# SSD scan: the outputs of two stages issued together, halves first, then carried states

## The chip, the cores and the metric

The kernel runs on one core of one Trainium2 chip. The metric is the device time of one execution in microseconds (us), as the median of several runs. The profile is one execution, recorded by the hardware profiler. Engines are named as there: PE is TensorE's matmul, PEld its weight load, DVE is VectorE, ACT ScalarE, POOL GpSimd, SP SyncE, whose queue issues most transfers.

## What is computed

One inference step of a two-layer streaming encoder, in float32, for 1024 prompt frames and 64 sample frames. Layer 0 is a Mamba-2 SSD mixer with a SwiGLU FFN, layer 1 banded attention with a SwiGLU FFN. The change touches the scan in the mixer alone. Cut to the scan, the reference is:

```python
CB = jnp.einsum('bcqgn,bcsgn->bcgqs', Cc, Bc)
y_diag = jnp.einsum('bcgjqs,bcsgjp->bcqgjp', CB[:, :, :, None] * Lm, xd)
chunk_states = jnp.einsum('bcsgn,bcsgjp->cbgjpn', Bc, xd * decay_to_end[..., None])
# scan over chunks: h -> h * chunk_decay + chunk_state; h_prev is the state ahead of each chunk
y_off = jnp.einsum('bcqgn,cbgjpn->bcqgjp', Cc, h_prev) * jnp.moveaxis(jnp.exp(Acs), -1, 2)[..., None]
y = (y_diag + y_off).reshape(b, L, SSM_HEADS, P)
```

After that come the skip term D, the gate silu(z), a norm for each of four groups, and the output projection.

## The kernel before

Frames lie along the free dimension: 1088 frames are three slices of 384, 384 and 320, and a slice is three chunks of up to 128. The 2048 inner channels are 16 tiles j of 128, two heads of 64 in each. One stage of the scan is a tile and a slice, q = 3 j + s, 48 stages in all.

PE's order is the program's order. It is written by a planner, the class Stream: the main line emits units of the input projection (24 matmuls mm for one weight tile and one slice, in two parts), and after each part a pump lets the side tasks run that are due. The planner has its own clock st.t, to which every unit and every step of a side task adds an estimated cost; a step is due after a delay and when a condition holds. `st.wait_for` lets that clock run on, without matmuls, until a condition holds. The other engines and SP's queue are ordered by the framework's scheduler.

A stage is the side task ssd_task(j, s), begun when the unit x of its tile and slice is out. Its steps are:

- load: MT and ea come from the decay rows in memory (L814, L817); DVE and ACT turn them into decays (L823 to L825). It needs C >= q - 3.
- A: three transposes xtp (L835), xd on DVE (L845), xe on POOL (L846), and MT times CB (L847). It needs C >= q - 1 and a gap of SSD_GAP = 4.4 after the last A.
- B, 6.0 later: six matmuls sp (L854), six updates hn of the carried state on DVE (L864, L867).
- C, 3.5 later: the outputs. Products of halves yp (L884, 12 matmuls in the profile, each 64 columns of the array, the two heads in the two halves), the products with the carried states yo (L893, six matmuls of 128 columns, four in the first stage of a tile), then y on DVE (L895), ea on DVE (L897), their sum on POOL (L898).
- D: y times z (L905), the transfer to memory (L906), squares for the norm. It needs z of the stage, and D in order.

The counters so["A"] to so["D"] hold how many stages have passed each step. The main line waits on them as well: unit x of stage q for C > q - 5, unit z for D > q - 3, unit C of a group for C. table_task (L683 to L713) makes the decay rows once, ahead of the first stage. PSUM has eight banks: two for mm, two for the small products (ax), four in the pool pyy for yp and yo. Buffers rotate by tag: xd 2, ea 3, h 6, y 6, halo 6.

Of the kernel before, what the change touches and what calls it, by code (L numbers as in the profile page):

```python
# [8 lines left out]
F32 = mybir.dt.float32  # L9
# [3 lines left out]
ALU = mybir.AluOpType  # L13
# [3 lines left out]
P = 128  # L17
D = 1024
# [5 lines left out]
SL = [(0, 384), (384, 384), (768, 320)]  # L24
# [5 lines left out]
CHL = [128] * 8 + [64]  # L30
# [15 lines left out]
SSD_GAP, SSD_D = 4.4, 8.0  # L46
# [35 lines left out]
C_D = 208  # L82
# [292 lines left out]
def hybrid_kernel(  # L375
# [5 lines left out]
    V, A, G, PE = nc.vector, nc.scalar, nc.gpsimd, nc.tensor  # L381
    ctx.enter_context(tc.manual_schedule(engines={mybir.EngineType.PE}))
    st = Stream()
# [49 lines left out]
    def col(c):  # L433
        return pcs[:, c:c + 1]
# [203 lines left out]
    with ExitStack() as es:  # L638
        pyy = es.enter_context(tc.tile_pool(reuse_waits="tile", name="pyy", bufs=4, space=PSUM))
        sb1 = es.enter_context(tc.tile_pool(reuse_waits="tile", name="sb1", bufs=1))  # L640
        sb2 = es.enter_context(tc.tile_pool(reuse_waits="tile", name="sb2", bufs=2))
# [33 lines left out]
        def table_task():  # L675
            ps = ax("dtn")
            for c in range(NCH):
                PE.matmul(ps[:, c * 32:(c + 1) * 32], dtT[c // 3][:64, (c % 3) * P:(c % 3 + 1) * P], stk, start=True, stop=True)
            with tc.high_priority(HIP):
                tt_ = [sb2.tile([P, 3, P], F32, tag=tg, bufs=2, name="tt") for tg in ("xe", "xe")]  # L680
                t0, t1 = (fl(t_)[:, :HW].rearrange("p (a b) -> p a b", b=HEADS) for t_ in tt_)
                t3 = dec
                V.tensor_tensor(t0, ps[:, :HW].rearrange("p (a b) -> p a b", b=HEADS), hb(pbs[:, 0:32]), op=ALU.add)  # L683
                V.scalar_tensor_tensor(fl(t1), fl(t0), -1.0, fl(t0), op0=ALU.mult, op1=ALU.min)
                A.activation(fl(t1), fl(t1), AF.Exp)
                V.tensor_scalar(fl(t3), fl(t1), LP[-1], None, op0=ALU.mult)
                for c_ in LP[-2::-1]:
                    V.scalar_tensor_tensor(fl(t3), fl(t3), c_, fl(t1), op0=ALU.add, op1=ALU.mult)
                V.scalar_tensor_tensor(fl(dt), fl(t0), 0.0, fl(t3), op0=ALU.max, op1=ALU.add)
                V.memset(dt[64:128, 8, :], 0.0)  # L690
                V.tensor_tensor(t0, dt, hb(negA), op=ALU.mult)
            yield 1.0, TB_V
            pa = ax("acsp")
            PE.matmul(pa[:, :HW], U, fl(t0), start=True, stop=True)
            with tc.high_priority(HIP):
                V.tensor_copy(fl(nac), pa[:, :HW])
            yield 0.5, 1.0
            pl_ = ax("lastp")
            PE.matmul(pl_[:, :HW], ones, fl(t0), start=True, stop=True)

            with tc.high_priority(HIP):
                for s, (o, n) in enumerate(SL):
                    ps = pyy.tile([P, 512], F32, tag="yy", name="acT")
                    for i in range(3):
                        c = 3 * s + i
                        L = CHL[c]
                        PE.transpose(ps[:32, i * P:(i + 1) * P], nac[:, c, :], ident)
                    row = sb2.tile([P, 384], F32, tag="xd", name="row")
                    A.copy(row[:32, :], ps[:32, :384])
                    nc.sync.dma_start(ac_[:, o:o + 384], row[:32, :])  # L710
                V.tensor_tensor(fl(dec), fl(nac), pl_[:, :HW], op=ALU.subtract)
                A.activation(fl(cd), pl_[:, :HW], AF.Exp, scale=-1.0)
                A.activation(fl(dec), fl(dec), AF.Exp)  # L713
            yield 1.7, 2.5
            tabs.append(1)
# [15 lines left out]
        class Conv:  # L731
# [5 lines left out]
            def __call__(self, s, ps_):  # L737
                ct = self.ct
                dst = self.dst[s] = sb2.tile([P, 384], F32, tag=self.tag, bufs=self.bufs, name=self.tag)
                raw = sb2.tile([P, 390], F32, tag="craw", bufs=4, name="craw")  # L740
                if s == 0:
                    G.memset(raw[:, 0:3], 0.0)
                else:
                    G.tensor_copy(raw[:, 0:3], self.prev[:, 0:3])
                if s < 2:
                    w_ = 384
                    scaled(raw[:, 3:387], ps_, s, 0, 384)
                    self.prev = sb2.tile([P, 4], F32, tag="halo", bufs=6, name="halo")
                    G.tensor_copy(self.prev[:, 0:3], raw[:, 384:387])
                else:  # L750
                    w_ = 323
                    G.tensor_copy(raw[:, 259:262], scs[:, ct, :])
                    scaled(raw[:, 3:259], ps_, s, 0, 256)
                    scaled(raw[:, 262:326], ps_, s, 256, 64)
                    G.tensor_copy(cst[:, ct, 0:3], raw[:, 256:259])
                    G.tensor_copy(cst[:, ct, 3:6], raw[:, 323:326])

                cw = C_CW + ct * 4
                A.activation(dst[:, :w_], raw[:, 0:w_], AF.Identity, bias=col(C_CB + ct), scale=col(cw))
                for k in range(1, 4):  # L760
                    V.scalar_tensor_tensor(
                        dst[:, :w_], raw[:, k:k + w_], col(cw + k), dst[:, :w_], op0=ALU.mult, op1=ALU.add
                    )
                if s < 2:
                    A.activation(dst[:, :384], dst[:, :384], AF.Silu)
                else:
                    A.activation(dst[:, 0:256], dst[:, :256], AF.Silu)
                    A.activation(dst[:, 256:320], dst[:, 259:323], AF.Silu)  # L768
                    A.activation(dst[:, 320:384], ident[:, 0:64], AF.Copy, scale=0.0)
# [30 lines left out]
        cb_done = []  # L800
        hst = {}
        so = dict(A=0, B=0, C=0, D=0, tA=0, tC=0)
        ssgs = {}

        def ssd_task(j, s):
            g, jj = divmod(j, 4)
            xsT = pair_t[j].dst[s]
# [4 lines left out]
            MT = sb2.tile([P, 2, 384], F32, tag="bp", bufs=4, name="MT")  # L812
            row = ac_.offset + 2 * j * NCH * P + o
            nc.sync.dma_start(MT, bass.AP(ac_.tensor, row, [[0, P], [NCH * P, 2], [1, 384]]))  # L814
            ea = sb2.tile([P, 384], F32, tag="ea", bufs=3, name="ea")
            for e in range(2):
                nc.sync.dma_start(ea[64 * e:64 * e + 64, :n], bass.AP(ac_.tensor, row + e * NCH * P, [[0, 64], [1, n]]))  # L817
            m3 = MT[:, :, :n]
# [5 lines left out]
            A.activation(m3, m3, AF.Exp, scale=-1.0)  # L824
            x = A.activation(ea[:, :n], ea[:, :n], AF.Exp, scale=-1.0)  # L825
            tc.add_manual_dep(x.ins, last.ins.name, AT, reason="one table load")
            yield 0, SSD_D, lambda: (g, s) in cb_done and so["A"] == q and so["C"] >= q - 1 and st.t >= so["tA"]
            Bn, CB = bc_t[g, s]
            if s == 2:
                h0 = sb2.tile([P, P], F32, tag="h0", bufs=1, name="h0")  # L830
# [2 lines left out]
            pt = ax("xtp")  # L833
            for i in range(3):
                PE.transpose(pt[:, i * P:(i + 1) * P], xsT[:, i * P:(i + 1) * P], ident)  # L835
            xd = sb2.tile([P, 3, P], F32, tag="xd", name="xd")
            xe = sb2.tile([P, 3, P], F32, tag="xe", name="xe")

            def hd(ap):
# [16 lines left out]
            for i in range(3):  # L856
# [2 lines left out]
                    hst[j] = h0  # L859
                h = hst.get(j)  # L860
                hs.append(h)
                hn = sb2.tile([P, P], F32, tag="h", bufs=6, name="hn")
                if c == 0:
                    V.tensor_copy(hn, sp[:, :P])  # L864
                else:
# [9 lines left out]
                if c == 8:  # L875
                    nc.sync.dma_start(hs_o[:, j * P:(j + 1) * P], hn)
            so["B"] = q + 1
            yield 0.8, 3.5, lambda: so["C"] == q and so["D"] >= q - 5 and st.t >= so["tC"]

            yp = pyy.tile([P, 512], F32, tag="yy", name="yp")  # L880
            for i in range(3):
                L = CHL[3 * s + i]
                for e in range(2):
                    PE.matmul(  # L884
                        yp[64 * e:64 * e + 64, i * P:i * P + L], xd[:, i, 64 * e:64 * e + 64],
                        MT[:, e, i * P:i * P + L], start=True, stop=True,
                    )
            yo = pyy.tile([P, 512], F32, tag="yy", name="yo")
            for i in range(3):
                c = 3 * s + i  # L890
                L = CHL[c]
                if c > 0:
                    PE.matmul(yo[:, i * P:i * P + L], hs[i], CT[:, i * P:i * P + L], start=True, stop=True)  # L893
            y = sb2.tile([P, 384], F32, tag="y", bufs=6, name="y")
            V.scalar_tensor_tensor(y[:, :n], xsT[:, :n], col(C_D + j), yp[:, :n], op0=ALU.mult, op1=ALU.add)  # L895
            q0 = P if s == 0 else 0
            V.tensor_tensor(ea[:, q0:n], yo[:, q0:n], ea[:, q0:n], op=ALU.mult)  # L897
            G.tensor_tensor(y[:, q0:n], y[:, q0:n], ea[:, q0:n], op=ALU.add)  # L898
            so["C"] = q + 1
            so["tC"] = st.t + SSD_GAP  # L900
            yield 1.5, 0, lambda: (j, s) in zst and so["D"] == q
            so["D"] = q + 1

            end = V if j == XT - 1 else G
# [50 lines left out]

        xss, done = [], []
        ssg0 = sb2.tile([P, NCH * P], F32, tag="ssg", bufs=1, name="x0")
        tags = [[], [("bp", 4)] * 4 + [("y", 6)] * 3 + [("ea", 3)], [("ea", 3)] + [("CT", 5)] * 2 + [("xd", 2)] * 2]
        for s, (o, n) in enumerate(SL):
            xs = []  # L960
            if s == 0:
# [1023 lines left out]
```

## Time and profile before

| what | value |
|---|---|
| median of 3 runs | 2992.34 us (2991.45 to 2995.91) |
| profiled execution | 2995.14 us, span 2993.4 us |
| mean granted clock of PE | 0.993 |
| DVE, ACT, POOL busy over the span | 68%, 48%, 24% |
| stages of the scan on PE, first xtp to last yo | 97.25 to 671.84 us, 48 stages |
| matmuls yp, yo, sp, xtp | 576, 256, 288, 144 |

Instructions of one kind in a row are merged in the timeline into one line with a count (x12); the first number is the start, the second the time to the end of the last. Idle time stands in brackets with what ended it; "issue" is time in which the engine waited for nothing that the profile shows. The ends of matmuls are modelled, so distances are taken from start to start.

### The profile page before, as it was taken

The page shows a single profiled execution, that of the slowest core. Times are in us where ns is not written, and L with a number is a line of the kernel's source. Part 1 is how long each engine was busy: PE and PEld are TensorE (multiplying, and loading weights), DVE is VectorE, ACT ScalarE, POOL GpSimd, SP SyncE. Part 2 cuts the span into 40 slices and gives each one's busy share as a digit, 9 for nine tenths or more (in the row PEclk, how much of TensorE's full clock was granted, in tenths as well). Part 3 has the DMA queues.
Part 4 walks back from the last instruction along what each step waited for, and adds up shares of the span by engine and source line. Part 5 has one row for each costly group of instructions (what it writes and reads, how often), then busy time and mean ns, then how long its engine had stood idle before and what let it go on. Part 6 is the DMA issues. An engine that isn't in the chain of part 4 may idle for free.

```text
span 2993.4 us, 56388 instructions
## 1 busy us (share of the span) xinstructions
PE 2935.9 (98%) x21626; PEld 2878.7 (96%) x21626; DVE 2039.4 (68%) x4471; ACT 1450.9 (48%) x2574; POOL 709.0 (24%) x821
## 2 busy tenths in 40 slices
PE   8899999999999999999999999999999999999999
PEld 7899999999999999999999899999999999999999
DVE  7788887876768554574557777777778655475544
ACT  6675666654453232244445566555654322244443
POOL 1233333330121433351111000000131343452111
PEclk9999999999999999999999999999999999999999
DMA  3333333334654222255655322222356222245654
GB/s 122 99 108 95 103 98 105 95 102 150 187 147 144 84 73 80 76 161 173 203 177 168 88 83 73 69 65 85 123 166 187 80 75 77 80 149 174 214 180 136
DMA packets 201550, 363.36 MB, mean 121 GB/s; under 512 B 20544, under 2 KB 149280, under 8 KB 201280
## 3 DMA queue, kind: packets, MB, share of 16 engines
q1 hardware_dynamic: 199488, 353.39, 38.1%
q0 software_dynamic: 1792, 6.36, 1.1%
q8 instruction: 170, 2.79, 0.4%
q14 instruction: 100, 0.82, 0.1%
HBM read 292.47 MB, written 62.74 MB: 119 GB/s over the span
## 4 chain that ended last, share of the span: by engine, by line
PE 83%; DVE 9%; DMA 4%; ACT 2%; issue 2%; POOL 0%; SPq 0%; DVEq 0%; ACTq 0%; POOLq 0%
PE px L1263 9%; PE px L1265 9%; PE px L1264 9%; PE mm L454 7%; PE mm L456 7%; PE mm L455 7%; PE po L1463 6%; PE po L1464 6%; PE po L1462 6%; PE mmx L455 3%; PE mmx L454 3%; PE mmx L456 3%; PE po L1746 2%; PE ptp L1707 1%; PE yp L884 1%
## 5 line engine op out<-in xcount | busy, mean ns | idle before, releaser
L454 PE MATMUL mm<-r,hl 128*128 128x384 f32 (+2 forms) x1664 | 557.9, 335 | 5.5 <-ACT BT L768 3.0
L456 PE MATMUL mm<-r,hl 128*128 128x384 f32 (+2 forms) x1664 | 540.3, 325 | 3.6 <-DVE hl L353 2.8
L455 PE MATMUL mm<-r,hl 128*128 128x384 f32 (+2 forms) x1664 | 539.2, 324 | 0.0
L341 DVE TENSOR_TENSOR hl<-raw,hl 128x1024 fp32r<-128x1024 f32 (+1 forms) x219 | 260.9, 1192 | 222.6 <-ACT hl L340 218.6
L1264 PE MATMUL px<-r,hl 128*128 128x288 f32 (+1 forms) x1184 | 347.6, 294 | 0.0
L454 PEld LDWEIGHTS mm<-r,hl 128*128 128x128 f32 x1664 | 316.1, 190 | 7.5 <-ACT BT L768 3.2
L456 PEld LDWEIGHTS mm<-r,hl 128*128 128x128 f32 x1664 | 315.2, 189 | 5.0 <-DVE hl L353 3.9
L455 PEld LDWEIGHTS mm<-r,hl 128*128 128x128 f32 x1664 | 316.5, 190 | 0.1
L1263 PE MATMUL px<-r,hl 128*128 128x288 f32 x1056 | 310.9, 294 | 0.0
L1265 PE MATMUL px<-r,hl 128*128 128x288 f32 x1056 | 310.7, 294 | 0.0
L340 ACT CAST hl<-raw 128x1024 fp32r<-128x1024 f32 (+1 forms) x219 | 219.9, 1005 | 177.5 <-PE po L1464 101.6
L480 POOL TENSOR_TENSOR ssum<-ssum,sq 128x256 f32<-128x256 f32 (+3 forms) x97 | 130.4, 1345 | 639.3 <-ACT sq L479 622.5
L1264 PEld LDWEIGHTS px<-r,hl 128*128 128x128 f32 x1184 | 222.6, 188 | 0.0
L1265 PE MATMUL px<-rx,hl 128*128 128x256 f32 x768 | 216.2, 282 | 4.5 <-DVE hl L341 4.5
L1263 PE MATMUL px<-rx,hl 128*128 128x256 f32 x768 | 216.7, 282 | 2.3 <-ACT hl L340 2.3
L1463 PE MATMUL po<-rx,hl 128*128 128x384 f32 (+1 forms) x624 | 201.6, 323 | 0.1
L1263 PEld LDWEIGHTS px<-r,hl 128*128 128x128 f32 x1056 | 198.4, 188 | 0.1
L1265 PEld LDWEIGHTS px<-r,hl 128*128 128x128 f32 x1056 | 198.3, 188 | 0.0
L1462 PE MATMUL po<-rx,hl 128*128 128x384 f32 (+1 forms) x608 | 197.4, 325 | 0.1
L1464 PE MATMUL po<-rx,hl 128*128 128x384 f32 (+1 forms) x608 | 196.5, 323 | 0.0
L1264 PE MATMUL px<-rx,hl 128*128 128x256 f32 x640 | 179.8, 281 | 0.0
L290 POOL TENSOR_TENSOR tt<-raw 128x512 f32<-128x512 f32 x40 | 56.0, 1399 | 439.3 <-DMA raw<-in_w_f_dram 362.9
(359 smaller groups left out, 8116.0 us busy)
## 6 DMA issues: line engine op xcount, KB each, us to landing
raw<-in_w_f_dram SPq DMA_DIRECT2D x154, 512.0 KB, 3.8
rx<-in_w_f_dram SPq DMA_DIRECT2D x54, 512.0 KB, 3.7
raw<-in_w_in_dram SPq DMA_DIRECT2D x40, 512.0 KB, 3.7
MT<-ascr SPq DMA_DIRECT2D x48, 384.0 KB, 3.8
sg<-hscr SPq DMA_DIRECT2D x88, 192.0 KB, 3.3
raw<-in_w_f_dram SPq DMA_DIRECT2D x44, 384.0 KB, 3.3
raw<-in_w_so_dram SPq DMA_DIRECT2D x32, 512.0 KB, 3.8
raw<-in_w_kv_dram SPq DMA_DIRECT2D x18, 512.0 KB, 3.5
```

What stands on the lines that cost most here:

```text
L340: self.nc.scalar.copy(h, v)
L341: (eng or self.eng or self.nc.vector).tensor_tensor(lo, v, h, op=ALU.subtract)
L454: PE.matmul(ps[:, :n], h_, xh, start=(first and i == 0), stop=False)
L455: PE.matmul(ps[:, :n], h_, xl, start=False, stop=False)
L456: PE.matmul(ps[:, :n], l_, xh, start=False, stop=(last and i == nk - 1))
L480: (eng or G).tensor_tensor(ssum[:, :n], ssum[:, :n], q[:, :n], op=ALU.add)
L1263: PE.matmul(ps, wh, ah[:, k, :], start=(k == 0), stop=False)
L1264: PE.matmul(ps, wh, al[:, k, :], start=False, stop=False)
L1265: PE.matmul(ps, wl, ah[:, k, :], start=False, stop=(k == 3))
L1462: PE.matmul(ps[:, :n], wh, xh, start=(k == 0), stop=False)
L1463: PE.matmul(ps[:, :n], wh, xl, start=False, stop=False)
L1464: PE.matmul(ps[:, :n], wl, xh, start=False, stop=(k == FT - 1))
```

## The change

The outputs of an even stage are not issued in its own step C. The stage is put on a list (held), and its task waits. The following odd stage puts itself there too, waits as C did, and calls the new function ssd_out: yp of both stages, then yo of both, then the work on DVE and POOL for each. C goes up by two at once, the cost is 3.0 for the pair where it was 1.5 for one, and D follows for both in order. Conditions are fitted to that: A needs C >= q - 2, the pair needs D >= q - 3. Buffers: xd 3, ea 4, h 9, y 4, halo 5. The decay rows in table_task use the tag of xd, and so have three buffers too.

```diff
-                    row = sb2.tile([P, 384], F32, tag="xd", name="row")
+                    row = sb2.tile([P, 384], F32, tag="xd", bufs=3, name="row")
...
-                    self.prev = sb2.tile([P, 4], F32, tag="halo", bufs=6, name="halo")
+                    self.prev = sb2.tile([P, 4], F32, tag="halo", bufs=5, name="halo")
...
+        held, ys = [], {}
+
+        def ssd_out():
+
+            banks = []
+            for j, s, xsT, CT, MT, ea, xd, hs in held:
+                yp = pyy.tile([P, 512], F32, tag="yy", name="yp")
+                banks.append([yp])
+                for i in range(3):
+                    L = CHL[3 * s + i]
+                    for e in range(2):
+                        PE.matmul(
+                            yp[64 * e:64 * e + 64, i * P:i * P + L], xd[:, i, 64 * e:64 * e + 64],
+                            MT[:, e, i * P:i * P + L], start=True, stop=True,
+                        )
+            for bk, (j, s, xsT, CT, MT, ea, xd, hs) in zip(banks, held):
+                yo = pyy.tile([P, 512], F32, tag="yy", name="yo")
+                bk.append(yo)
+                for i in range(3):
+                    L = CHL[3 * s + i]
+                    if 3 * s + i > 0:
+                        PE.matmul(yo[:, i * P:i * P + L], hs[i], CT[:, i * P:i * P + L], start=True, stop=True)
+            for (yp, yo), (j, s, xsT, CT, MT, ea, xd, hs) in zip(banks, held):
+                n = SL[s][1]
+                y = ys[j, s] = sb2.tile([P, 384], F32, tag="y", bufs=4, name="y")
+                V.scalar_tensor_tensor(y[:, :n], xsT[:, :n], col(C_D + j), yp[:, :n], op0=ALU.mult, op1=ALU.add)
+                q0 = P if s == 0 else 0
+                V.tensor_tensor(ea[:, q0:n], yo[:, q0:n], ea[:, q0:n], op=ALU.mult)
+                G.tensor_tensor(y[:, q0:n], y[:, q0:n], ea[:, q0:n], op=ALU.add)
+            held.clear()
...
-            ea = sb2.tile([P, 384], F32, tag="ea", bufs=3, name="ea")
+            ea = sb2.tile([P, 384], F32, tag="ea", bufs=4, name="ea")
...
-            yield 0, SSD_D, lambda: (g, s) in cb_done and so["A"] == q and so["C"] >= q - 1 and st.t >= so["tA"]
+            yield 0, SSD_D, lambda: (g, s) in cb_done and so["A"] == q and so["C"] >= q - 2 and st.t >= so["tA"]
...
-            xd = sb2.tile([P, 3, P], F32, tag="xd", name="xd")
+            xd = sb2.tile([P, 3, P], F32, tag="xd", bufs=3, name="xd")
...
-                hn = sb2.tile([P, P], F32, tag="h", bufs=6, name="hn")
+                hn = sb2.tile([P, P], F32, tag="h", bufs=9, name="hn")
...
-            yield 0.8, 3.5, lambda: so["C"] == q and so["D"] >= q - 5 and st.t >= so["tC"]
-
-            yp = pyy.tile([P, 512], F32, tag="yy", name="yp")
...
-            so["C"] = q + 1
-            so["tC"] = st.t + SSD_GAP
-            yield 1.5, 0, lambda: (j, s) in zst and so["D"] == q
+            held.append((j, s, xsT, CT, MT, ea, xd, hs))
+            if q % 2 == 0:
+                yield 0.8, 0, lambda: so["C"] > q and (j, s) in zst and so["D"] == q
+            else:
+                yield 0.8, 3.5, lambda: so["C"] == q - 1 and so["D"] >= q - 3 and st.t >= so["tC"]
+                ssd_out()
+                so["C"] = q + 1
+                so["tC"] = st.t + SSD_GAP
+                yield 3.0, 0, lambda: (j, s) in zst and so["D"] == q
+            y = ys.pop((j, s))
```

The list of buffers that take the first inputs at the start (tags) follows the new counts of y, ea and xd.

More of the change, by code (lines that the diff above doesn't have):

```diff
@@ L877, in ssd_task @@
             so["B"] = q + 1
-            yield 0.8, 3.5, lambda: so["C"] == q and so["D"] >= q - 5 and st.t >= so["tC"]
-            yp = pyy.tile([P, 512], F32, tag="yy", name="yp")
[L881 to L898, printed above, removed]
-            so["C"] = q + 1
-            so["tC"] = st.t + SSD_GAP
-            yield 1.5, 0, lambda: (j, s) in zst and so["D"] == q
+            held.append((j, s, xsT, CT, MT, ea, xd, hs))
[8 more added lines that the diff above has]
+            y = ys.pop((j, s))
             so["D"] = q + 1
@@ L957, in hybrid_kernel @@
         ssg0 = sb2.tile([P, NCH * P], F32, tag="ssg", bufs=1, name="x0")
-        tags = [[], [("bp", 4)] * 4 + [("y", 6)] * 3 + [("ea", 3)], [("ea", 3)] + [("CT", 5)] * 2 + [("xd", 2)] * 2]
+        tags = [[], [("bp", 4)] * 4 + [("y", 4)] * 3 + [("ea", 4)], [("ea", 4)] + [("CT", 5)] * 2 + [("xd", 3)] * 2]
         for s, (o, n) in enumerate(SL):
```

## Prediction

> **What bounds the kernel now.** I read the page first, then the busy times by stretch, then the waits of TensorE (PE), then the tiles that the change touches, then the timeline of PE.
>
> ```profile
> span 2993.4 us, 56388 instructions
> PE 2935.9 (98%) x21626; PEld 2878.7 (96%) x21626; DVE 2039.4 (68%) x4471; ACT 1450.9 (48%) x2574; POOL 709.0 (24%) x821
> ```
>
> PE is the bound of the whole. The scan lies between 97 and 672 us, so the same is asked of that stretch, with its start (97 to 112) apart:
>
> ```profile
> 97.00:112.00 15.00, 6.88 (x41) 6.01 (x41) 10.87 (x31) 7.74 (x10) 1.62 (x2) 0.69 0.30 94
> 380.00:535.00 155.00, 154.50 (x1078) 149.53 (x1078) 126.98 (x322) 97.43 (x137) 53.14 (x94) 1.00 0.33 101
> 97.00:672.00 575.00, 559.70 (x3902) 538.63 (x3901) 472.19 (x1204) 355.51 (x504) 201.48 (x336) 0.99 0.33 102
> ```
>
> The columns are length, then busy time of PE, PEld, DVE, ACT and POOL, then the granted clock. In the middle PE is busy 154.5 of 155 us, DVE 127 of 155 (82%). Only the start has holes: PE is busy 6.88 of 15 us, at a clock of 0.69. The waits of PE between 97 and 672 say the same; the first three:
>
> ```profile
> PE sp L854 <- POOL xe L846: 4.4, 1, 4.4
> PE yp L884 <- DVE MT L847: 3.8, 1, 3.8
> PE nbp L517 <- DVE xd L845: 2.7, 1, 2.7
> ```
>
> Each is a single wait, and the first two lie at the start (their rows are below). So outside the start a change to the scan is worth what it takes off PE's own queue, and costs what it makes PE wait.
>
> **The change part by part.** (1) *Fewer changes between halves and whole.* A stage's 12 yp matmuls are 64 columns wide, in two halves of the array; everything around them is 128 wide. This is one stage late in the scan, first PE, then its weight loads (PEld), then a stretch without halves:
>
> ```profile
> 627.56 0.33 PE L455 MATMUL mm<-r,hl 128*128 128x384 f32 x1
> 627.73 0.34 PE L456 MATMUL mm<-r,hl 128*128 128x384 f32 x1
> 628.00 0.88 PE L884 MATMUL yp<-MT,xd 128*64 128x128 f32 x12
> 628.80 0.94 PE L893 MATMUL yo<-CT,hn 128*128 128x128 f32 x6
> 629.58 0.49 PE L835 MATMUL xtp<-ident,xsT 128*128 128x128 f32 x3
> ...
> 628.00 0.64 PEld L884 LDWEIGHTS yp<-MT,xd 128*64 128x64 f32 x12 [0.25 <-issue]
> 628.80 0.74 PEld L893 LDWEIGHTS yo<-CT,hn 128*128 128x128 f32 x6 [0.17 <-issue]
> ...
> 604.57 0.34 PE L456 MATMUL mm<-r,hl 128*128 128x384 f32 x1
> 604.74 0.49 PE L835 MATMUL xtp<-ident,xsT 128*128 128x128 f32 x3
> 605.07 0.83 PE L854 MATMUL sp<-xe,Bn 128*128 128x128 f32 x6
> ```
>
> From one mm to the next, or from mm to xtp, PE takes 0.17 us (627.56 to 627.73, 604.57 to 604.74); from mm to yp it takes 0.27. Three whole matmuls take 0.33 (604.74 to 605.07), 0.11 each. The 12 loads of yp last 0.64, in six pairs, so 0.11 a pair. Without changes of width, the stretch from the last mm to xtp would be 0.17 + 6 x 0.11 + 6 x 0.11 = 1.49; it is 629.58 - 627.73 = 1.85. One way in and out costs 0.36, about 0.35. PEld shows where: nothing is loaded for 0.25 ahead of yp and 0.17 ahead of yo. That this holds for all stages, the tiles' idle times show (first yp's, then yo's):
>
> ```profile
>   issue: 10.5, 47
> ...
>   issue: 4.3, 24
> ```
>
> 0.22 us at each of 47 entries, and 0.18 at 24 exits of 48; the other exits are put down to engines that had long finished. The new order is yp, yp, yo, yo for two stages: 24 ways in and out instead of 48. I take 24 x 0.35 = **-8.4 us**. Bounds: only the entry's 0.10 saved, -2.4; both idle times of PEld (0.42) saved, -10.1. The matmuls themselves, their count and the planner's cost (2 x 1.5 against 3.0) stay.
>
> (2) *The start.* The unit x of stage 5 waits in the planner for `so["C"] > q - 5`. C used to go up by one; now it goes from 0 to 2, so both first stages must be out ahead of that unit. PE now:
>
> ```profile
> 97.25 0.82 PE L835 MATMUL xtp<-ident,xsT 128*128 128x128 f32 x6
> 102.43 1.34 PE L854 MATMUL sp<-xe,Bn 128*128 128x128 f32 x6 [4.36 <-POOL xe L846]
> 107.53 1.55 PE L884 MATMUL yp<-MT,xd 128*64 128x128 f32 x12 [3.75 <-DVE MT L847]
> 110.02 1.49 PE L854 MATMUL sp<-xe,Bn 128*128 128x128 f32 x6
> 111.80 0.61 PE L454 MATMUL mm<-r,hl 128*128 128x320 f32 x1
> ```
>
> The second sp and the third xtp (110.02 to 111.80, 1.78 us) follow the first yp; in the new order they come ahead of it, inside the second wait. That is worth up to -1.8. Against it, the second stage's yo loses the cover of a unit (111.80 on) and needs the states of its own stage: six updates of 0.27 after sp:
>
> ```profile
> L867 DVE SCALAR_TENSOR_TENSOR hn<-hn,cd,sp 128x64 f32<-128x64 f32 x224 | 50.3, 273 | 2.2 <-PE sp L854 1.8
> ```
>
> 1.6 us if DVE has them last. (3) *The third buffer of xd, for the rows.* The decay rows go to memory in three transfers, and the loads of MT follow on SP's queue:
>
> ```profile
> 84.94 0.81 SPq L710 DMA_DIRECT2D ascr<-row  x2
> 86.97 0.38 SPq L814 DMA_DIRECT2D MT<-ascr  x1
> 89.56 0.31 SPq L710 DMA_DIRECT2D ascr<-row  x1
> 92.00 0.39 SPq L814 DMA_DIRECT2D MT<-ascr  x1
> 96.16 0.59 SPq L814 DMA_DIRECT2D MT<-ascr  x1
> ...
> 99.26 1.27 DVE L823 TENSOR_SCALAR MT<-MT,nac 128x128 f32<-128x128 f32 x6 [1.81 <-DMA MT<-ascr]
> ```
>
> The third row goes out 4 us after the others, since it has to wait for a buffer, and the second MT only at 92.00. With three buffers it can follow directly (about 86); the later loads move up by up to 3.5 us, and with them the DVE queue that stood at 99.26 for such a load and that both waits of PE go back to. DVE has other work there (10.87 of 15 us), so not all of it arrives. For (2) and (3) together I take **-3.0**, nearer to the hidden 1.8 than to the sum 1.8 + 3.5; ends -5.3 and +1.6. The fourth ea buffer puts two more transfers on SP's queue here, ahead of later loads; SP's gaps above hold them.
>
> (4) *Waits of the planner elsewhere.* An odd stage's A step and its load of MT need the same outputs as before, and its output comes as long after its sp as before; so no later step is moved back by its odd predecessor. For an even stage, x and A need no more than before; the load of MT needs the output of the stage three back instead of four, about two stages before it asks. For odd stages x needs the stage four back instead of five. Only at x of stage 7 does this come ahead of the old order, by half a unit (12 mm of 0.17, 2 us): no PE work is lost, priced at nothing; if its states were late it would cost the 1.6 above once. y with four buffers: an output needs the multiplication by z of the stage four before, which is two z units older. Free; and h with nine buffers is seven live states for a pair.
>
> (5) *Two outputs at once on DVE and POOL.* Each stage has these:
>
> ```profile
> L895 DVE SCALAR_TENSOR_TENSOR y<-xsT,pcs,yp 128x384 f32<-128x384 f32 (+1 forms) x48 | 28.1, 585 | 2.1 <-PE yp L884 1.7
> L897 DVE TENSOR_TENSOR ea<-yo,ea 128x384 f32<-128x384 f32 (+2 forms) x47 | 22.7, 484 | 0.8 <-PE yo L893 0.7
> L898 POOL TENSOR_TENSOR y<-y,ea 128x384 f32<-128x384 f32 (+2 forms) x47 | 46.3, 985 | 85.2 <-DVE ea L897 85.1
> ```
>
> Their sum stays; a pair puts 2 x (0.585 + 0.484) = 2.14 us in a row on DVE, 1.07 more than now. Behind it stand the copy of mm, xd and hn. A unit is 24 mm of 0.17, 4.1 us, and has two banks, so a copy may be 1 us late: free in mid-scan. At the end of the scan the last two stages share the queue with the next part's loads, and I put **+1.0** (0 to 2.1) there.
>
> Sum: -8.4 - 3.0 + 1.0 = **-10.4 us**. The profiled execution took 2995.14 us (span 2993.4), so 2984.7; the median of the runs shown is 2992.34, which gives **2982 us**.
>
> **The rivals.** *DVE becomes the wall (slower).* Four banks of pyy hold exactly one pair, and DVE is at 82%. If xd of the next stage queues behind the pair's 2.14 us and its xtp bank (of two) isn't free when PE comes to the next transposes, PE stands for the added 1.07 us at each pair: 24 x 1.07 = +25.7, net +15.3, 3008 us. It decides from 10.4 / 24 = 0.43 us a pair. For it: DVE's 82%. Against it: in 380 to 535 PE lacks 0.5 us in all, over some 13 stages (48 in 575 us), so the present order leaves room. The Trainium skill (TensorEngine Tiling (Array Packing), PSUM Bottleneck) warns that tiling quickens TensorE but not the copying out of PSUM, which can then be the bound. By that rule the change would lose as in this rival; the trace so far speaks against it, since the only wait of PE on DVE for yp is the one at the start. Chance 0.13.
>
> *The start gets worse.* If both first outputs wait for the last MT and for the second stage's states, the two waits stay and a third as long as the second (3.75 us) comes, and the matmuls after it run slow: sp's six take 1.34 after a wait and 0.83 at 605.07, 0.5 more, and two such groups follow. That is 3.75 + 1, some +5, in place of -3: -8.4 + 5 + 1 = -2.4, 2990 us. The Trainium skill (TensorE: Matmul & The Clock Gate, "Why this matters for your kernels") says to leave no idle gap of over about 3 us, or the clock falls back; the trace agrees, with 0.69 in 97 to 112 against 1.00 later. Chance 0.08.
>
> *The change of width isn't what costs.* The loads ahead of yp and yo might stand for the four-bank release or the 64-wide load itself, and come back inside a pair (yp to yp, yo to yo). Then at most the entry's -2.4 is left, and small gains and losses at start and end cancel: 2990 us. Against it: 47 entries with the same 0.22. Chance 0.11.
>
> **How the numbers follow.** The forecast has the remaining 0.68. What a measurement of this kernel can tell from no change is 0.2%, 6 us. Forecast: faster. The start and the width rival: within. DVE: slower. So 0.68 / 0.19 / 0.13. The forecast's own ends are -10.1 - 5.3 = -15.4 (2977) and about -5 (2987); the range goes from 2976 up to 2993, to hold the two middle rivals at 2990 with the 3 us by which single runs differ from their median, and leaves out the slower one.
>
> **What would show it.** Right: yp groups of 24 matmuls on PE, followed by yo groups of up to 12; yp's idle time on PEld for "issue" near 24 entries and 5 us; the third row's transfer behind the first two; the second wait at the start shorter, the first unit after it before 111.8. Wrong: new waits of PE on DVE or POOL in mid-scan (xtp, sp or mm on xd, hn or craw), or a start stretch that ends after 115 us; a gain that lies after 700 us would not be mine.

## The result, and the profile after

The changed kernel took 2979.82 us (median of 4 runs, 2975.27 to 2982.1), the kernel before 2991.89 beside it (4 runs, 2989.7 to 2995.91). The ratio is 0.9956, 95% interval 0.9944 to 0.9968: 12.1 us faster, at a forecast of 10.4. The page of the changed kernel, then its busy times in the three stretches shown of before, then its longest waits of PE between 97 and 672 us:

```profile
span 2978.0 us, 56302 instructions
PE 2921.0 (98%) x21626; PEld 2871.4 (96%) x21626; DVE 2040.2 (69%) x4471; ACT 1394.1 (47%) x2530; POOL 719.2 (24%) x821
...
97.00:112.00 15.00, 10.63 (x76) 9.87 (x77) 13.12 (x37) 5.78 (x9) 6.42 (x7) 0.77 0.35 98
380.00:535.00 155.00, 153.00 (x1080) 149.77 (x1079) 126.03 (x323) 81.39 (x125) 57.05 (x94) 1.00 0.32 99
97.00:672.00 575.00, 559.83 (x3985) 545.97 (x3986) 483.55 (x1238) 303.91 (x477) 215.91 (x338) 0.99 0.34 105
...
PE xtp L866 <- DVE nv L498: 4.8, 6, 0.8
PE sp L885 <- POOL xe L877: 3.7, 1, 3.7
PE nst L487 <- DVE nv L499: 2.7, 1, 2.7
PE sp L885 <- DVE xd L876: 1.8, 1, 1.8
```

Three things differ from before. The start is fuller (PE busy 10.63 of 15 us instead of 6.88). The middle is not: PE has lost 2 us of 155 where it had lost 0.5, and a row heads the list that was small before, xtp behind nv, six times 0.8 instead of three times 0.4 (the row of before is below). And ACT is busy 51.6 us less over the scan (303.91 instead of 355.51), though the change touches no step of ACT.

```profile
PE xtp L835 <- DVE nv L498: 1.3, 3, 0.4
```

The new order stands as announced: yp in groups of 24, yo in groups of ten or twelve. PEld's idle time for "issue" is about halved ahead of yp (10.5 before) and down by a third ahead of yo (4.3 before):

```profile
  issue: 5.4, 24
...
  issue: 2.9, 16
```

The start, on PE and on SP's queue:

```profile
99.56 0.94 PE L885 MATMUL sp<-xe,Bn 128*128 128x128 f32 x6 [3.68 <-POOL xe L877]
...
102.63 1.62 PE L885 MATMUL sp<-xe,Bn 128*128 128x128 f32 x6 [1.82 <-DVE xd L876]
104.18 2.83 PE L816 MATMUL yp<-MT,xd 128*64 128x128 f32 x24
...
109.42 0.39 PE L454 MATMUL mm<-r,hl 128*128 128x320 f32 x1
...
82.75 1.27 SPq L710 DMA_DIRECT2D ascr<-row  x3
...
86.47 0.53 SPq L845 DMA_DIRECT2D MT<-ascr  x1
```

The three rows go out together, the second MT at 86.47 instead of 92.00, the second wait is 1.82 instead of 3.75, and the first unit after it starts at 109.42 instead of 111.80 (of these 2.4 us, 2.2 were there ahead of the first stage, as the table below shows). But by then the change has issued the outputs of two stages and before those of one. At the mm of 117.88 in before, where both have issued two, the lead is 4.87 us, so the start has gained 2.7.

**Where the time lies.** The same matmul of the projection can be found in every trace. For example, these two are the same, at the end of the first group of stages, in before and after, so the lead there is 11.05 us:

```profile
219.43 0.34 PE L454 MATMUL mm<-r,hl 128*128 128x384 f32 x1
...
208.38 0.41 PE L454 MATMUL mm<-r,hl 128*128 128x384 f32 x1
```

The table gives how the lead over before grows between such marks, named by their times in before (negative is gained). "Ahead" is the lead already there at 93.74, where the order of PE is the same in all kernels: that column is chance. (e_nst9 and e_nst9_10 are the same kernel up to far behind that mark, and stand at -0.7 and -5.3.) The last column is the difference of the spans.

| kernel | ahead | 94 to 219 | 219 to 641 | 641 to 727 | whole span |
|---|---|---|---|---|---|
| the change | -2.2 | -8.9 | -0.8 | -2.0 | -15.4 |
| the change again (e_pair) | -3.7 | -8.6 | -0.8 | -1.9 | -15.1 |
| e_alt | -4.1 | -8.4 | +3.8 | -1.8 | -11.1 |
| e_weave | -2.1 | +1.5 | +17.0 | +2.2 | +16.6 |
| e_single01 | -3.5 | -9.5 | -1.3 | -0.7 | -15.9 |
| e_row2 | +0.1 | -6.2 | -1.3 | -1.4 | -9.9 |
| e_rows_only | -2.0 | -2.3 | 0.0 | +1.3 | -0.8 |
| e_ea_only | -1.3 | -6.4 | -0.1 | -3.7 | -12.7 |
| e_buffers | -2.2 | -6.4 | -0.5 | -4.0 | -11.5 |
| e_nst9 | -0.7 | -9.0 | -7.0 | -2.1 | -20.5 |
| e_before_nst9 | -3.7 | -1.3 | -1.4 | +2.3 | -1.5 |
| e_nst9_10 | -5.3 | -9.4 | -8.0 | -2.5 | -26.9 |

Three cautions. The profile of before is an execution of 2995.14 us, 3.3 above the median beside the change, so 15.4 us between the profiles is too much. And e_before_nst9 shows 1.3 in the second column and gains nothing by its times, so some 1 to 2 us of that column are chance too.

The third is the clock of PE, which falls behind some waits. In before the granted clock is 0.50 from 162 to 164 and from 660 to 662, behind the waits of PE near 158 and 656. The mm stand 0.32 us apart there instead of 0.17:

```profile
660.39 0.52 PE L455 MATMUL mm<-r,hl 128*128 128x384 f32 x1
660.71 0.52 PE L456 MATMUL mm<-r,hl 128*128 128x384 f32 x1
```

Eleven mm are spaced like that each time, so such a stretch costs some 1.6 us beside the wait. It does not come each time: e_before_nst9 has the same two waits near 155 as before has near 158 (0.8 and 0.8, against 1.0 and 0.8) and keeps a clock of 1.00 there. Between 140 and 727 before has two such stretches, the change one (0.50 from 672 to 674), e_ea_only and e_buffers none.

What the table does show is the surprise: 32 of the 48 stages have their outputs between 219 and 641 (384 of the 576 matmuls yp of before), and the change gains 0.8 us there.

### The profile page after: what moved, and what is told of

Read it like the earlier page. It is cut to its first block, busy times and chain, and to the rows that moved or that the text cites. A ratio compares the mean times of both kernels' runs of the same rounds, so it can differ in the third digit from the quotient of the medians.

```text
span 2978.0 us, 56302 instructions
## 1 busy us (share of the span) xinstructions
PE 2921.0 (98%) x21626; PEld 2871.4 (96%) x21626; DVE 2040.2 (69%) x4471; ACT 1394.1 (47%) x2530; POOL 719.2 (24%) x821
## 4 chain that ended last, share of the span: by engine, by line
PE 83%; DVE 9%; DMA 3%; ACT 2%; issue 2%; POOL 0%; SPq 0%; DVEq 0%; ACTq 0%; POOLq 0%
PE px L1280 9%; PE px L1281 9%; PE px L1282 9%; PE mm L454 7%; PE mm L456 7%; PE mm L455 7%; PE po L1480 6%; PE po L1481 6%; PE po L1479 6%; PE mmx L455 3%; PE mmx L454 3%; PE mmx L456 3%; PE po L1763 2%; PE ptp L1724 1%; DVE sc L1702 1%
```

## The experiments

Every kernel was timed beside runs of before on the same chip; "difference" is that of the two medians. Rows with the same median of before share a chip; rows on different chips are best compared by their ratios.

| kernel | us (runs) | before | difference | ratio, 95% interval |
|---|---|---|---|---|
| e_pair | 2979.98 (5) | 2990.42 | -10.4 | 0.9961 [0.9948, 0.9973] |
| e_alt | 2986.90 (11) | 2990.42 | -3.5 | 0.9985 [0.9976, 0.9994] |
| e_row2 | 2983.41 (9) | 2990.42 | -7.0 | 0.9972 [0.9962, 0.9982] |
| e_rows_only | 2992.61 (11) | 2990.42 | +2.2 | 1.0001 [0.9992, 1.001] |
| e_weave | 3010.55 (4) | 2991.51 | +19.0 | 1.0063 [1.0049, 1.0077] |
| e_ea_only | 2983.85 (9) | 2991.51 | -7.7 | 0.9978 [0.9968, 0.9987] |
| e_nst9 | 2971.52 (5) | 2991.51 | -20.0 | 0.9937 [0.9923, 0.995] |
| e_before_nst9 | 2992.46 (11) | 2991.51 | +1.0 | 1.0005 [0.9996, 1.0014] |
| e_buffers | 2982.76 (7) | 2991.06 | -8.3 | 0.9973 [0.9962, 0.9983] |
| e_single01 | 2979.14 (5) | 2991.06 | -11.9 | 0.9961 [0.9948, 0.9975] |
| e_nst9_10 | 2971.34 (5) | 2991.06 | -19.7 | 0.9936 [0.9923, 0.9948] |

One execution of e_weave took 9095 us and is left out of its row.

**The ways in and out of halves.** e_pair is the changed kernel unaltered. e_alt keeps all of it, the pairs and the buffers, and puts back the alternation inside a pair: yp, yo, yp, yo.

> The changed kernel again, for a second profile on the same chip as the others. All theories: 10 to 14 us under the kernel before. Theory 1 (the gain sits at the start of the scan and little of it in the middle, where the 0.35 us a pair that the joined halves save is eaten by transposes that wait after the norm's transposes): the distance between the two kernels grows by 7 to 10 us up to the first group's end (about 219 us of before) and by under 1 us in each of the next two groups; six waits of about 1 us of xtp. Theory 2 (the gain is the halves, spread over all 24 pairs, and the start of the profile was chance): some 2 us in each group, and the lead ahead of the first stage (2.2 us in the first profile) may be gone.

> As the changed kernel, two stages issued at once, but in the order yp, yo, yp, yo: 48 ways in and out of halves instead of 24, everything else the same. If a way in and out costs 0.35 us: 24 x 0.35 = 8.4 us more than the changed kernel, some 4 us under the kernel before, with 47 or 48 entries of idle time for issue at yp on PEld. If the halves aren't what saves (rival: only issuing two stages at once and the buffers matter): within 2 us of the changed kernel.

```diff
                 yp = pyy.tile([P, 512], F32, tag="yy", name="yp")
-                banks.append([yp])
+                yo = pyy.tile([P, 512], F32, tag="yy", name="yo")
+                banks.append([yp, yo])
...
-            for bk, (j, s, xsT, CT, MT, ea, xd, hs) in zip(banks, held):
-                yo = pyy.tile([P, 512], F32, tag="yy", name="yo")
-                bk.append(yo)
                 for i in range(3):
                     L = CHL[3 * s + i]
                     if 3 * s + i > 0:
```

e_alt is 6.9 us slower than e_pair, on intervals that don't meet. The same pair on PE, first e_alt, then e_pair, from the last mm ahead of it to the first behind it:

```profile
441.87 0.34 PE L456 MATMUL mm<-r,hl 128*128 128x384 f32 x1
442.14 0.88 PE L817 MATMUL yp<-MT,xd 128*64 128x128 f32 x12
442.94 0.94 PE L824 MATMUL yo<-CT,hn 128*128 128x128 f32 x6
443.81 0.77 PE L817 MATMUL yp<-MT,xd 128*64 128x128 f32 x12
444.51 0.71 PE L824 MATMUL yo<-CT,hn 128*128 128x128 f32 x4
...
445.20 0.42 PE L454 MATMUL mm<-r,hl 128*128 128x384 f32 x1
```

```profile
440.04 0.34 PE L456 MATMUL mm<-r,hl 128*128 128x384 f32 x1
440.30 1.43 PE L816 MATMUL yp<-MT,xd 128*64 128x128 f32 x24
441.66 1.38 PE L826 MATMUL yo<-CT,hn 128*128 128x128 f32 x10
...
443.02 0.42 PE L454 MATMUL mm<-r,hl 128*128 128x384 f32 x1
```

The alternation takes 445.20 - 441.87 = 3.33 us, the pair 443.02 - 440.04 = 2.98: 0.35 for one way in and out. Over the 12 pairs between 219 and 528 the same distances, from the last matmul ahead of the pair to the first behind it, sum to 38.75 us and 34.82: 3.93 in all, 0.33 each. The Trainium skill (TensorEngine Tiling (Array Packing), "Key Properties") says that a change of tiling mode drains TensorE; the trace agrees that a change costs, and 0.33 is what it measures for a way in and out.

e_weave goes the other way, in the kernel before: yp and yo alternate chunk by chunk within a stage, 128 ways in and out instead of 48.

> The kernel before with more ways in and out of halves: yp and yo by chunks (yp, yo, yp, yo, yp, yo), all else the same. Stages with three yo have three ways in and out instead of one (32 stages), those with two have two (16): 80 more. At 0.33 us each (what the two orders of a pair differ by in PE's steps, 3.92 us for 12 pairs): +26 us over the kernel before. If an entry alone costs (0.10): +8 us. If a way in and out costs nothing when the rest of PE is full: 0.

```diff
             yp = pyy.tile([P, 512], F32, tag="yy", name="yp")
+            yo = pyy.tile([P, 512], F32, tag="yy", name="yo")
...
-                L = CHL[3 * s + i]
+                c = 3 * s + i
+                L = CHL[c]
...
-            yo = pyy.tile([P, 512], F32, tag="yy", name="yo")
-            for i in range(3):
-                c = 3 * s + i
-                L = CHL[c]
```

It lost 19.0 us, 0.24 for each of the 80. The table shows why it isn't the full 26. Between 219 and 641 it lost 17.0, which is near the full price for the some 53 ways added in these 32 stages (0.32 each), and at the end 2.2 for the some 7 of the last four stages, near the full price again. Only in 94 to 219 it lost no more than 1.5 for 20 ways. There the two waits of xtp for ACT near 158 (1.0 and 0.8 us) are gone from its trace, and so is the half-clock stretch behind them: the slower yp filled time in which PE would have waited.

**The start.** e_single01 is the change with the outputs of stages 0 and 1 issued singly, as before.

> The changed kernel with the first two stages issued one by one (yp, yo, then yp, yo with a unit between), pairs from stage 2 on. The prediction gave the start's new order (the second sp and the third xtp inside the second wait, both outputs ahead of the unit) 1.8 us of gain. If so: 1.5 to 2.5 us more than the changed kernel (1.8 and one more way in and out, 0.33), a second wait at the start of about 2 us longer with less in it. If the start gains by the buffers alone: within 1 us of the changed kernel.

```diff
-            if q % 2 == 0:
+            if q < 2:
+                held.pop()
+                yield 0.8, 3.5, lambda: so["C"] == q and so["D"] >= q - 3 and st.t >= so["tC"]
+                held.append((j, s, xsT, CT, MT, ea, xd, hs))
+                ssd_out()
+                so["C"] = q + 1
+                so["tC"] = st.t + SSD_GAP
+                yield 1.5, 0, lambda: (j, s) in zst and so["D"] == q
+            elif q % 2 == 0:
```

2979.14 us, the change's own time (same ratio, 0.9961): the new order of the start is worth nothing. e_row2 takes the third row's own buffer out of the change, e_rows_only puts the third buffer of xd, for the rows and the stages, into the kernel before (with halo at five, as in the change).

> The changed kernel with two buffers for the three decay rows, as before: the third row goes into the first one's. If the third buffer brought the loads of MT forward: the second MT goes out some 3.5 us later again, the first wait at the start grows by 2 to 4 us, and the time is 2 to 4 us over the changed kernel. If the start gains from the order alone: within 1 us of it.

> The kernel before with the third buffer of xd alone (rows and scan), nothing paired. If the buffer brings the start forward: 2 to 4 us under the kernel before, with the first two waits of PE (4.4 and 3.8 us) shorter. If it needs the pairing: no change within 1 us.

```diff
+            rows_ = []
...
-                    row = sb2.tile([P, 384], F32, tag="xd", bufs=3, name="row")
+                    if s < 2:
+                        rows_.append(sb2.tile([P, 384], F32, tag="xd", bufs=3, name="row"))
+                    row = rows_[s % 2]
```

```diff
-                    row = sb2.tile([P, 384], F32, tag="xd", name="row")
+                    row = sb2.tile([P, 384], F32, tag="xd", bufs=3, name="row")
...
-            xd = sb2.tile([P, 3, P], F32, tag="xd", name="xd")
+            xd = sb2.tile([P, 3, P], F32, tag="xd", bufs=3, name="xd")
```

In the change the buffer is worth about 3.4 us (2983.41 against 2979.98, intervals that overlap), alone it is worth nothing that the times show (the interval leaves room for 2.4). Its trace shows the step itself, though: the wait of yp for MT is 1.4 us instead of 3.8, and up to the first unit behind it the lead grows by 3.6:

```profile
PE yp L884 <- DVE MT L847: 1.4, 1, 1.4
```

Of these 3.6, 2.3 are left at 219, after new waits of yo for hn (2.4 and 1.0 in all), and 1.0 at 727. e_row2's queue of SP and its first outputs:

```profile
85.07 0.81 SPq L713 DMA_DIRECT2D ascr<-row  x2
...
89.69 0.31 SPq L713 DMA_DIRECT2D ascr<-row  x1
...
92.10 0.38 SPq L848 DMA_DIRECT2D MT<-ascr  x1
...
107.83 2.83 PE L819 MATMUL yp<-MT,xd 128*64 128x128 f32 x24 [1.82 <-DVE MT L881]
```

The second MT is late again (92.10), and since both first yp stand together, the pair waits 1.82 for its MT. Up to the mm of 117.88 e_row2 gains 0.6 us, the change 2.7 (2.4 in e_pair), e_single01 2.8. So what the start gains seems to come with the buffer, in the old order as in the new. It is no proof, for e_ea_only gains 2.4 up to there without that buffer.

**The buffers.** e_buffers is the kernel before with all of the change's buffers but h's, e_ea_only with the fourth buffer of ea alone (and halo at five, which e_rows_only has too, without a gain); PE's order in both is that of before, instruction by instruction.

> The kernel before with a fourth buffer of ea alone. Theory (ACT waited for the load of ea, which waited for its buffer, and so had to load a table for MT and another for ea; xtp of stage 7 waited 1.8 us for ACT): some 20 to 45 table loads of 1.28 us fewer on ACT in the scan, and the two waits of xtp on ACT (1.0 and 0.8 us) near 155 us gone: 1 to 3 us under the kernel before. Rival (the table loads fall because the loads of MT come in pairs): as many table loads as before, no change.

> The kernel before with the buffers of the change and no pairing: ea 4, xd 3 (rows too), y 4 with its condition D >= q - 3, halo 5; PE's order is the kernel before's, instruction by instruction. Theory (about two thirds of the gain are buffers, above all ea's): 7 to 10 us under the kernel before, the lead made up to 219 us and after 640 us, none between; table loads on ACT as few as with ea alone. What the pairing then adds is 2 to 4 us (7.8 saved in ways in and out, 4 lost in waits after the norm's transposes). Rival (the buffers help only because a pair needs them): within 3 us of the kernel before, or of ea alone at most.

```diff
-                    self.prev = sb2.tile([P, 4], F32, tag="halo", bufs=6, name="halo")
+                    self.prev = sb2.tile([P, 4], F32, tag="halo", bufs=5, name="halo")
...
-            ea = sb2.tile([P, 384], F32, tag="ea", bufs=3, name="ea")
+            ea = sb2.tile([P, 384], F32, tag="ea", bufs=4, name="ea")
```

(e_buffers also has xd with three buffers, the rows among them, and y with four and D >= q - 3.) They gain 7.7 and 8.3 us. By the medians ea's buffer alone is some two thirds of what the whole change gains; by the ratios (0.9978 against 0.9961 and 0.9956) it is about half. The traces name the two places. In before, ACT's queue came to L825 ahead of the load of ea, which waits for a buffer; the first two lines below are ACT, the next two PE, and the last four the same at the end of the scan:

```profile
156.26 0.47 ACT L825 ACTIVATE ea<-ea 128x320 f32<-128x320 f32 x1 [2.91 <-DMA ea<-ascr]
...
158.04 0.42 ACT L767 ACTIVATE xsT<-xsT 128x256 f32<-128x256 f32 x1
...
158.51 0.44 PE L835 MATMUL xtp<-ident,xsT 128*128 128x128 f32 x2 [0.99 <-ACT xsT L767]
159.75 0.33 PE L835 MATMUL xtp<-ident,xsT 128*128 128x128 f32 x1 [0.80 <-ACT xsT L769]
...
652.61 1.28 ACT L825 ACT_TABLE_LOAD   x1 [2.28 <-DMA ea<-ascr]
...
654.28 0.37 ACT L520 ACTIVATE rb<-nbp 128x256 f32<-128x256 f32 x1
...
654.79 0.91 PE L854 MATMUL sp<-xe,Bn 128*128 128x128 f32 x6 [1.01 <-ACT rb L520]
...
658.35 0.43 PE L517 MATMUL nbp<-ident,rst 128*128 128x128 f32 x2 [2.65 <-DVE xd L845]
```

In e_ea_only the same steps of the end, ACT, then PE:

```profile
643.64 0.38 ACT L520 ACTIVATE rb<-nbp 128x256 f32<-128x256 f32 x1 [1.88 <-PE nbp L517]
...
645.87 0.83 PE L854 MATMUL sp<-xe,Bn 128*128 128x128 f32 x6
...
648.12 0.43 PE L517 MATMUL nbp<-ident,rst 128*128 128x128 f32 x2 [1.42 <-DVE xd L845]
```

ACT no longer stands for ea ahead of rb (its 1.88 here are for nbp), and the first wait is gone, the second down from 2.65 to 1.42. The lead of e_ea_only over before grows by 4.05 us between 152.56 and 180.94 and by 4.01 between 637.07 and 666.62, and hardly between. The waits themselves are 1.8 us of the first (0.99 and 0.80) and 2.2 of the second (1.01, and 1.23 of the 2.65); most of the rest are the two half-clock stretches of some 1.6 us each, which e_ea_only doesn't have. The two places together are 8.1, the times give 7.7. Its trace gains 2.4 more ahead of 118, but it is the fastest of its nine runs (2982.42), and where these come from isn't shown.

**The norm's transposes.** The six waits of xtp for nv look like this in the change, first; in e_nst9 the norm of a stage comes 9 instead of 12 of the planner's us after its squares, second:

```profile
240.26 0.83 PE L885 MATMUL sp<-xe,Bn 128*128 128x128 f32 x6
240.93 0.49 PE L487 MATMUL nst<-ident,ssg 128*128 128x128 f32 x3
242.22 0.52 PE L866 MATMUL xtp<-ident,xsT 128*128 128x128 f32 x3 [0.80 <-DVE nv L498]
```

```profile
239.29 0.49 PE L487 MATMUL nst<-ident,ssg 128*128 128x128 f32 x3
...
241.71 0.83 PE L885 MATMUL sp<-xe,Bn 128*128 128x128 f32 x6
242.37 0.49 PE L866 MATMUL xtp<-ident,xsT 128*128 128x128 f32 x3
```

sp, nst and xtp all use the two banks of ax. With three in a row both banks are taken when PE comes to xtp, and it waits until DVE has read one (here nst's, by nv); with mm between nst and sp, as in e_nst9, there is no wait.

> The changed kernel with one number changed: the norm's transposes (nst) come 9.0 instead of 12.0 of the planner's time after a stage's last step, for the first three groups. In PE's order they then stand alone, and no longer as the third of sp, nst, xtp (or nst, sp, xtp) in a row with two banks for all three. If those waits ate the mid-scan gain: the six waits of 1.07 us (less 0.11 for a normal step) and the three of 0.35 go, 6 x 0.96 + 3 x 0.24 = 6.5 us less than the changed kernel, and the lead over the kernel before grows by about 2.5 us in each middle group instead of 0.5. Rival (the steps only wait elsewhere, since DVE is behind): within 2 us of the changed kernel, with as much waiting of PE on DVE.

> The same number changed in the kernel before, nothing paired. There three waits of 0.76 and three of 0.35 us stand in a row of that kind: 3 x 0.59 + 3 x 0.24 = 2.5 us at most. If the waits are a matter of the pairing: 0 to 2.5 us under the kernel before. If the earlier transposes are a gain of their own: as much as in the changed kernel, some 6 us.

> The version with 9.0 for the norm's transposes, and 10.0 instead of 5.0 for the last group, where two of them and a third stand in a row at the end of the scan (waits of 2.96 and 1.07 us in the changed kernel's profile). If the two banks are the cause there too: those two waits shorter by 2 to 3.5 us, 22 to 24 us under the kernel before. Rival (DVE is behind there with the next part's inputs, and PE meets it one step later): within 1.5 us of the version with 9.0 and 5.0.

```diff
             if jj == 3:
-                yield 0, 12.0 if g < 3 else 5.0
+                yield 0, 9.0 if g < 3 else 5.0
```

e_nst9_10 has 10.0 in place of the 5.0 too; e_before_nst9 is the same edit as above in the kernel before. e_nst9 takes 2971.52 us, the best median but for e_nst9_10, which no measurement here tells from it; 8.5 under e_pair's (9.6 by the differences, 7.2 by the ratios, for they were timed on different chips). Between 219 and 641 it gains 6.2 us more than the change, and the row of xtp behind nv is gone from its waits. In before the same number gains nothing: there the waits were three, 1.3 us in all. e_nst9_10 was to take away the wait of nst (2.7) at the end of the scan as well, and only moved it:

```profile
PE nbp L517 <- DVE rst L511: 3.6, 1, 3.6
```

## Why the prediction was right, and where only its sum was right

Direction and size were right, but not term by term. Errors of both signs partly cancelled: the largest single gain, ea's buffer, was not in the sum, and the new waits for the norm were not either. That 10.4 came so near to 12.1 is luck in that part.

| term | forecast | what the runs show |
|---|---|---|
| (1) ways in and out | -8.4 | -7.9 (24 x 0.33; e_alt 6.9) |
| (2) order of the start | with (3) -3.0 | 0 (e_single01) |
| (3) third buffer of xd, rows | with (2) -3.0 | 0 alone by the times, -3.6 at the start of its trace; about -3.4 inside the change |
| ea's fourth buffer | 0 | -7.7 alone (e_ea_only) |
| (4) waits of the planner elsewhere | 0 | +3.5 by the waits of xtp for nv (4.8 against 1.3) |
| (5) two outputs at once | +1.0 | about +2 at the end, behind the norm's transposes; 0 in mid-scan |

With -8.3 for the buffers together that makes -10.7, and -13.5 if the 2.8 are added by which the rows' buffer is worth more inside the change (3.4) than all other buffers are on top of ea's (0.6); measured were 12.1, 10.4 and, in e_single01, 11.9. The traces of the change and e_buffers agree stretch by stretch. In 94 to 219 the change is 2.5 us ahead, for six pairs at 0.33. From 219 to 641 it is 0.3 ahead: sixteen pairs save 5.2, and xtp waits 4.8 for nv instead of 0.7. At the end it is 2.0 behind.

(1) The step held: price, place and number. The rival that width isn't what costs falls: by it e_alt would equal e_pair.

(2) failed, (3) held only in part. 1.78 us of PE work did move into the second wait, but nothing came of it: with the old order kept, the time is the same. The forecast took a hole in PE's queue as time to be filled; what sets the end of the start, as far as the waits show, is DVE's chain to MT and xd, which the order of PE doesn't shorten. The buffer's step in (3) is in the traces as forecast, a shorter wait for MT, and the 2.7 us that the change gains up to 117.88 are near the 3.0; that it gave nothing alone in the times was not forecast. The rival of a worse start came in e_row2, as a third wait, of 1.82 instead of 3.75; the third buffer keeps it out of the change.

The sentence on ea's buffer is the worst one: it counted the two transfers that the buffer adds and not the waits that it ends. The waits were in the trace of before; the tile ea shows, as those who waited, ACT's table loads and activations:

```profile
  ACT L825: 10.6, 11
  ACT ea L825: 6.8, 4
```

That is 17.4 us of ACT standing, which the prediction did not ask for, ACT being busy half the time. It cost PE 8 at the two places where the next thing in ACT's queue was xsT or rb, for which PE waited; about 3 of these 8 are the half clock behind the waits.

(4) failed in its own words, "no later step is moved back": it followed the loads, x, A and C, and left out D, which by the program now comes for two stages together and has the norm behind it. In the trace nst stands right between sp and xtp twice a group. It is the sign named for a wrong forecast, a new wait of PE on DVE in mid-scan, with another cause. That it eats much of the gain of (1) there is shown by e_nst9.

(5) DVE did not become the wall. Between 380 and 535 it is busy 126.03 us (126.98 before), and the waits of PE there are two of 0.8 on nv and one of 0.3 on craw, none on xd or hn; the rule that the Trainium skill states on this (TensorEngine Tiling (Array Packing), PSUM Bottleneck) does not decide here. At the end the term was too small: from 641 to 727 e_buffers gains 4.0 and the change 2.0, though two pairs lie there. The longest of the waits is nst behind nv, and the half-clock stretch of 672 to 674, some 1.4 us more, follows it:

```profile
669.29 0.52 PE L487 MATMUL nst<-ident,ssg 128*128 128x128 f32 x3 [2.69 <-DVE nv L499]
```

So the loss there goes through the norm, as in (4); that it comes from two outputs in a row on DVE isn't shown.

What stays open: e_pair and e_buffers are not told apart by their intervals, so that the new order gains 2 us beyond the buffers is the difference of two medians, no more. Nearer is e_single01, on the same chip as e_buffers and with pairs from stage 2 on: 3.6 us less, five runs from 2976.69 to 2981.99 against seven from 2979.40 to 2983.98. With the norm out of the way it gains: the intervals of e_nst9 lie below those of e_before_nst9 and e_buffers. The buffers with 9.0 and the old order were not run. Whether e_nst9 gains more than the 6.2 seen in mid-scan is open: the times say 7 to 10, by what one compares. Why the clock fell behind some waits and not behind others is open too.

## What to carry to other kernels

A change that brings buffers along is two changes: run the buffers alone, in the old order, before crediting the order. A late load at the head of an in-order queue is priced by what stands behind it in that queue and who waits for that, not by the engine's busy share; and a wait can cost nearly twice its length when the clock falls behind it. And when steps are regrouped, follow the last link too (here D and the norm): a gain of 0.33 us a pair is lost to one wait of 0.8 or more for a bank every third pair, and is got back by moving that one step.

## What the runs showed of the hardware

With ea's buffer, ACT has fewer loads of its function table at L825: 29 fall to 9. Before, then e_ea_only:

```profile
L825 ACT ACT_TABLE_LOAD x29 | 37.2, 1283 | 11.0 <-DMA ea<-ascr 10.6
...
L825 ACT ACT_TABLE_LOAD x9 | 11.5, 1283 | 0.2
```

Each takes 1.283 us; the Trainium skill (ScalarE: Activation LUTs, "What ACT_TABLE_LOAD costs") gives about 1283 ns for the load, and the traces agree. But at L824 the loads rise from 26 to 40, so over the scan 110 loads fall to 99 only, in e_ea_only as in e_buffers, and ACT is busy 346.64 and 345.99 us instead of 355.51. The change has 66 loads. So most of the 51.6 us by which ACT is less busy there comes with the issuing in pairs and not with the buffer; e_alt, with pairs in the other order, has 301.88. What part of the pairing regroups ACT's work was not looked into.

The waits of PE near 158 in before, 1.0 and 0.8 us, were followed by a granted clock of 0.50 and the loss of some 1.6 us; 0.8 and 0.8 in e_before_nst9 were not. So the price of a wait is read from the mm behind it as well.

And executions of kernels whose PE order is the same up to 93.74 us are up to 5 us apart at that mark: a difference that one pair of profiles shows ahead of the edit is no part of its effect.
